# A two-layer encoder trunk: turning the output between the layers on VectorE and through device memory instead of on TensorE

## The chip, the cores and the metric

The kernel runs on one core of one Trainium2 chip. The metric is the device time of one launch in microseconds. One core has TensorE (matrix multiplications into PSUM; its weight loads are listed apart as PEld), VectorE (DVE), ScalarE (ACT), GpSimd (POOL), and SyncE (SP), which here issues most transfers between device memory and the on-chip memory SBUF. The engines run side by side, each through its own instructions in order, and wait for one another by semaphores.

## The reference

A trunk of two layers over one sequence of 256 rows and 2048 columns, in float32. Each layer is one mixer with three head groups fed by one input projection, then a residual and a LayerNorm:

```python
def hybrid_layer(x, mem, w_in, rel_table, gate_w, gate_b, gla_norm_g, w_mem_kv, w_out, ln_g, ln_b):
    h = x @ w_in
    a_q, a_k, a_v, a_z, b_q, b_k, b_v, b_z, b_lr, m_q, m_z = jnp.split(h, cuts, axis=-1)
    y_a = chunk_band_attention(a_q, a_k, a_v, rel_table)
    o_b = gla_chunk_recurrence(b_q, b_k, b_v, log_g)          # log_g from b_lr; then an RMS norm
    mk, mv = jnp.split(mem @ w_mem_kv, 2, axis=-1)
    y_m = memory_attention(m_q, mk, mv)
    y = concat([y_a * silu(a_z), y_b * silu(b_z), y_m * silu(m_z)])
    return layer_norm(DEEPNORM_ALPHA * x + y @ w_out, ln_g, ln_b)

def reference(x, mem, ...):
    h = x
    for l in range(2):
        h = hybrid_layer(h, mem, w_in[l], ...)
    return h
```

(Reshapes and some arguments are left out.) What matters here is the seam between the layers: the output of layer 0 is both the input of the big projection of layer 1 and its residual.

## The kernel before

**Products.** Every float32 operand is split into a high part (a cast to float32r) and a low part (the remainder), and a product is made of three matmuls: high by high, low by high, high by low. ScalarE makes the high part and VectorE the low part (`parts`, L114 to L117). All matmuls are recorded at L93.

**Weights.** The weights stream from device memory in pieces of 128 partitions x 1024 elements (512 KB), one per call of `piece` (L128 to L143): a load by SyncE into a `raw` buffer, then `wh` by ScalarE and `wl` by VectorE. There are four buffers each of `raw`, `wh` and `wl`. A piece is 16 or so matmuls. Groups of eight pieces follow each other; `as_group` puts the activations on the stationary side, `ws_group` the weights (two halves of four pieces).

**Order.** The orders of TensorE and SyncE are the order of the program text (L49); those of ScalarE and VectorE are planned when the kernel is built, where `piece` has a high priority (AHEAD, 4000) and `transposed` one of AHEAD // 4 for its scaling and splitting. Small jobs such as attention heads are generators: `tick` runs the next step of a waiting one after each weight piece, and the number that a step yields is how many pieces later the next one is due. At most two are active at once.

**The seam.** After the last output group of layer 0, `norm_between` (L627 to L642) normalises the sum in place in `res` (two tiles of 128 rows x 2048 columns) without the LayerNorm's gain and offset. Layer 1 then runs group MV of the memory projection (`as_group`, eight pieces), group MK (`ws_group`, eight pieces), and BQK, the first group that multiplies the layer's own input. For that input the columns have to lie on the partitions: 16 blocks of 128 columns, four to a quarter, each quarter an `operand` (`xq[q]`) of high and low parts. Five such operand buffers exist, and the four of the memory input `memq` are still read by MK.

`transposed` (L574 to L600) does the turning, started just ahead of MK and finished before BQK (L779, `finish(gens[:1])`). It first turns gain and offset into per-partition columns (`gT`, L578 and L579). Then in each of eight steps TensorE turns four blocks of 128x128 of `res` into a PSUM bank (L590), ScalarE and VectorE scale them with gain and offset into a scratch buffer (L596, L598), and `parts` writes the quarter's high and low halves. One step follows each MK piece. `restored` later applies gain and offset to `res` itself for the residual (L607, L608).

Of the kernel before, what the change touches and what calls it, by code (L numbers as in the profile page):

```python
# [8 lines left out]
F32 = mybir.dt.float32  # L9
# [3 lines left out]
AF = mybir.ActivationFunctionType  # L13
ALU = mybir.AluOpType
# [4 lines left out]
P = 128  # L19
D = 2048  # L20
T = 256
# [11 lines left out]
AHEAD = 4000  # L33
# [3 lines left out]
def hybrid_trunk_kernel(  # L37
# [7 lines left out]
    pe, dve, act, pool, sp = nc.tensor, nc.vector, nc.scalar, nc.gpsimd, nc.sync  # L45
# [27 lines left out]
    def enter(name, bufs=1, **kw):  # L73
        return ctx.enter_context(tc.tile_pool(name=name, bufs=bufs, **kw))
# [4 lines left out]
    wp = enter("wp", 4)  # L79
    hd = enter("hd", 1)  # L80
    sc = enter("sc", 8)
    sm = enter("sm", 1)
    psd = enter("psd", 2, space=bass.MemoryType.PSUM)
    psa = enter("psa", 4, space=bass.MemoryType.PSUM)

    uid = [0]

    def nm(s):
        uid[0] += 1
        return f"{s}_{uid[0]}"  # L90
# [4 lines left out]
    def bank():  # L95
        return psa.tile([P, 512], F32, name=nm("bk"), tag="bk")

    def scratch(shape, dtype=F32):
        return sc.tile(shape, dtype, name=nm("sc"), tag="sc")
# [4 lines left out]
    ident = cst.tile([P, P], F32, name="ident")  # L104
    lmask = cst.tile([P, 6, CH], U8, name="lmask")
    eye = cst.tile([P, CH], F32, name="eye")
    eps = cst.tile([P, 2], F32, name="eps")

    def operand():

        x = opp.tile([P, 4, 2, T], F32R, name=nm("x"), tag="x")
        return x[:, :, 0], x[:, :, 1], x.rearrange("p j h t -> p j (h t)")

    def parts(hi, lo, src):  # L114

        act.copy(hi, src)  # L116
        dve.tensor_tensor(lo, src, hi.bitcast(F32), op=ALU.subtract)  # L117
# [456 lines left out]
    def transposed(xq, gbT):  # L574

        raw, gT = gbT
        pt = bank()
        pe.transpose(pt[:, :P], raw, ident)  # L578
        dve.tensor_copy(gT, pt[:, :32])  # L579
        for q in range(4):  # L580
            x = operand()
            hi, lo, _ = x
            xq.append(x)
            for j in range(0, 4, 2):
                pt = bank()
                y = scratch([P, 2, T])
                for jj in range(2):
                    kt = q * 4 + j + jj
                    for t in range(2):
                        pe.transpose(pt[:, jj * T + t * P:jj * T + (t + 1) * P], res[:, t, kt * P:(kt + 1) * P], ident)  # L590
                with tc.high_priority(AHEAD // 4):
                    for jj in range(2):
                        kt = q * 4 + j + jj
                        src, g, b = pt[:, jj * T:(jj + 1) * T], gT[:, kt:kt + 1], gT[:, 16 + kt:17 + kt]
                        if jj == 0:
                            act.activation(y[:, jj], src, AF.Identity, bias=b, scale=g)  # L596
                        else:
                            dve.tensor_scalar(y[:, jj], src, g, b, op0=ALU.mult, op1=ALU.add)  # L598
                    parts(hi[:, j:j + 2], lo[:, j:j + 2], y)
                yield 1  # L600

    def restored(gb):

# [10 lines left out]
    def wo_pieces(l, n):  # L614

        if n < 3:
            return [w512[l, G_WO + n, pc] for pc in range(8)]
        return [[w256[l, i, pc // 2][:, pc % 2 * 512:pc % 2 * 512 + 512] for i in range(2)] for pc in range(8)]
# [137 lines left out]
    res = per.tile([P, 2, D], F32, name="res")  # L756
# [3 lines left out]
    for l in range(L):  # L760
        mk = [per.tile([P, 4, T], F32R, name=nm("mk"), tag=f"mk{i}") for i in range(2)]
        mv = [per.tile([P, 2, 512], F32R, name=nm("mv"), tag=f"mv{i}") for i in range(2)]
        xq = []
        if l == 0:
            def each(p):
                if p in (2, 4, 6, 7):
                    xq.append(resident_quarter(len(xq), xT[len(xq)]))

            first_memory(mk, mv, each)
        else:  # L770
            memq = []
            parts(*mv, as_group(w512[l, G_MV], memq, 512, 2, memT))
            gens = [transposed(xq, gbT), restored(gb)]
            waiting.append(gens[0])
            for i, a, b in ws_group(w512[l, G_MK], memq):
                tmp = scratch([P, 2, T])
                total(tmp, a, b)
                parts(mk[0][:, i:i + 2], mk[1][:, i:i + 2], tmp)
            finish(gens[:1])  # L779
# [21 lines left out]
        def heads(g):  # L801
            t = hd.tile([P, 4, T], F32, name=nm("qk"), tag="qk", bufs=4)
            for i, a, b in ws_group(w512[l, g], xq):
                total(t[:, i:i + 2], a, b)
            return t
# [12 lines left out]
        bias = {}  # L818
# [12 lines left out]
        for half in range(2):  # L831
            values(2 + half)
            q = heads(G_AQ0 if half == 0 else G_AQ1)
            k = heads(G_AK0 if half == 0 else G_AK1)
            gens.append([a_head(half * 4 + h, load_bias, bias, q[:, h], k[:, h], asv, yraw[1 + half][:, h]) for h in range(4)])
            waiting.extend(gens[-1])
        q = [hd.tile([P, 4, T], F32R, name=nm("mq"), tag="qk", bufs=4) for _ in range(2)]
# [15 lines left out]
        for i, g in ((1, G_AZ0), (2, G_AZ1), (3, G_MZ)):  # L853
            y = operand()
# [18 lines left out]
        for n in range(WO_N):  # L873
            if last:
                g, b = scratch([P, 512]), scratch([P, 512])
            else:
                both = per.tile([P, 2, 512], F32, name=nm("gb"), tag=f"yr{n}")
                g, b = both[:, 0], both[:, 1]
# [3 lines left out]
            src = wo_pieces(l, n)  # L882
# [122 lines left out]
```

## Time and profile before

| | |
|---|---|
| time of three runs, median (lowest to highest) | 925.73 us (925.34 to 926.28) |
| the profiled execution's own time | 925.59 us |
| its span, from first to last instruction | 923.8 us |
| granted TensorE clock, mean | 0.998 |
| bytes read and written in device memory | 175.77 MB and 2.10 MB |
| the eight steps of turning on TensorE (L590) | 482.3 to 505.6 us |

The time of an execution is 1.8 us more than its span. The profile lists for each engine how long it was busy, and a chain of work followed back from the last instruction: at each step to what released it, or to the instruction before it on its engine. Rows of a group give `out<-in`, partitions x elements, a count, busy time, the mean time of one in ns, and the idle time before them with what ended it. In a timeline the first number is the start in us from the span's start and the second the duration. "SPq" is the queue of instructions of SyncE. DMA rows give the size and the median time from issue to landing.

### The profile page before, as it was taken

How to read it: one execution, taken by the hardware profiler on the slowest of the kernel's cores; microseconds unless marked ns; L12 is line 12 of the kernel's file. 1: busy time of each engine (PE TensorE's matmuls, PEld its weight loads, DVE VectorE, ACT ScalarE, POOL GpSimd, SP SyncE). 2: the span in 40 equal slices, each digit the busy share in tenths (PEclk: the TensorE clock that was granted, in tenths of full speed). 3: DMA queues.
4: the chain of work that ended last, by engine and by line, in shares of the span. 5: the costliest groups of instructions: out<-in, count | busy, mean ns of one | idle time of the engine just before them, and what ended most of it. 6: DMA issues, size and time to landing. Idle time of an engine off the chain costs nothing.

```text
span 923.8 us, 14249 instructions
## 1 busy us (share of the span) xinstructions
PE 916.7 (99%) x5500; PEld 806.5 (87%) x5500; DVE 587.9 (64%) x812; ACT 498.2 (54%) x714; POOL 21.8 (2%) x49
## 2 busy tenths in 40 slices
PE   9999999999999999999999999999999999999997
PEld 7889998998888888888888899889888888888885
DVE  6764478665564666555587666975655555766566
ACT  6644485484454675433566445754744555754350
POOL 1000000000000000000000000000000000110000
PEclk9999999999999999999999999999999999999999
DMA  9955865546554566756675466546555544667652
GB/s 306 334 189 174 306 207 173 161 165 194 183 162 160 171 206 200 219 193 196 227 249 164 150 205 204 193 154 196 170 193 166 164 152 160 199 222 223 198 163 92
DMA packets 71253, 178.85 MB, mean 194 GB/s; under 512 B 7304, under 2 KB 31240, under 8 KB 70928
## 3 DMA queue, kind: packets, MB, share of 16 engines
q1 hardware_dynamic: 69120, 173.30, 57.1%
q0 software_dynamic: 1920, 4.36, 1.8%
q8 instruction: 43, 0.70, 0.3%
q10 hardware_dynamic: 144, 0.26, 0.1%
q14 instruction: 26, 0.21, 0.1%
HBM read 175.77 MB, written 2.10 MB: 193 GB/s over the span
## 4 chain that ended last, share of the span: by engine, by line
PE 98%; DMA 0%; DVE 0%; ACT 0%; SPq 0%; issue 0%
PE acc L93 89%; PE bk L93 8%; PE bk L526 1%; DMA raw<-w 0%; PE bk L561 0%; PE bk L590 0%; PE bk L494 0%; PE bk L393 0%; SPq L177 0%; ACT res L746 0%; ACT wh L116 0%; DVE stats L731 0%; PE bk L340 0%; DVE res L730 0%; DVE res L682 0%
## 5 line engine op out<-in xcount | busy, mean ns | idle before, releaser
L117 DVE TENSOR_TENSOR wl<-raw,wh 128x1024 fp32r<-128x1024 f32 (+3 forms) x321 | 370.0, 1154 | 255.9 <-ACT wh L116 254.9
L116 ACT CAST wh<-raw 128x1024 fp32r<-128x1024 f32 (+3 forms) x321 | 318.7, 994 | 329.9 <-PE acc L93 236.5
L93 PE MATMUL acc<-x,wh 128*128 128x512 f32 x1248 | 398.0, 400 | 0.1
L93 PE MATMUL acc<-wh,x 128*128 128x512 f32 (+2 forms) x1236 | 357.3, 370 | 0.1
L93 PEld LDWEIGHTS acc<-x,wl 128*128 128x128 f32 x1248 | 234.4, 188 | 55.3
L93 PEld LDWEIGHTS acc<-wh,x 128*128 128x128 f32 x1236 | 227.0, 188 | 27.9 <-ACT wh L116 0.6
L93 PE MATMUL acc<-x,wl 128*128 128x256 f32 x1248 | 246.0, 278 | 0.0
L93 PE MATMUL acc<-wl,x 128*128 128x512 f32 (+2 forms) x618 | 228.0, 369 | 0.0
L93 PEld LDWEIGHTS acc<-x,wh 128*128 128x128 f32 x1248 | 192.0, 189 | 1.9 <-ACT wh L116 0.4
L93 PEld LDWEIGHTS acc<-wl,x 128*128 128x128 f32 x618 | 116.0, 188 | 15.0 <-DVE wl L117 0.9
L518 ACT ACTIVATE sc<-sc,mx 128x128 f32<-128x128 f32 (+1 forms) x32 | 14.4, 450 | 20.3 <-DVE mx L516 20.3
L511 DVE SCALAR_TENSOR_TENSOR sc<-bk,bias 128x384 f32<-128x384 f32 x16 | 8.9, 554 | 12.7 <-PE bk L93 12.7
L382 ACT ACTIVATE sc<-sc 128x512 f32<-128x512 f32 x12 | 7.6, 633 | 12.5 <-DVE sc L380 12.5
L117 DVE TENSOR_TENSOR x<-sc,x 128x512 fp32r<-128x512 f32 x20 | 13.3, 684 | 0.7 <-ACT x L116 0.7
L116 ACT CAST x<-raw 128x1024 fp32r<-128x1024 f32 x5 | 5.3, 1053 | 15.3 <-DMA raw<-memT 12.7
L117 DVE TENSOR_TENSOR x<-res,x 128x512 fp32r<-128x512 f32 (+2 forms) x14 | 10.5, 765 | 4.2 <-ACT x L116 4.1
L93 PE MATMUL bk<-qk,qk 128*128 128x128 f32 (+1 forms) x64 | 13.1, 326 | 0.0
L117 DVE TENSOR_TENSOR x<-raw,x 128x1024 fp32r<-128x1024 f32 x5 | 6.1, 1225 | 10.9 <-ACT x L116 10.9
L93 PE MATMUL bk<-sc,asv 128*128 128x256 f32 (+1 forms) x64 | 13.0, 326 | 0.0
L262 DVE SCALAR_TENSOR_TENSOR sc<-acc,sc 128x512 f32<-128x512 f32 x19 | 12.9, 681 | 0.0
L116 ACT CAST x<-sc 128x512 fp32r<-128x512 f32 x20 | 11.8, 615 | 1.3 <-DVE sc L598 1.3
L623 DVE SCALAR_TENSOR_TENSOR res<-res,acc 128x512 f32<-128x512 f32 x15 | 9.7, 684 | 4.2 <-PE acc L93 4.2
(209 smaller groups left out, 567.8 us busy)
## 6 DMA issues: line engine op xcount, KB each, us to landing
raw<-w SPq DMA_DIRECT2D x214, 512.0 KB, 3.9
raw<-w SPq DMA_DIRECT2D x64, 388.0 KB, 3.3
raw<-w SPq DMA_DIRECT2D x83, 256.0 KB, 3.2
bias<-relw SPq DMA_DIRECT2D x16, 192.0 KB, 4.1
res<-xT SPq DMA_DIRECT2D x4, 512.0 KB, 5.0
res<-xn SPq DMA_DIRECT2D x1, 2048.0 KB, 8.2
raw<-memT SPq DMA_DIRECT2D x4, 512.0 KB, 4.3
res<-memT SPq DMA_DIRECT2D x6, 256.0 KB, 6.1
```

The lines of the kernel that those rows point to most:

```text
L93: pe.matmul(o, l, r, start=start, stop=stop, skip_group_check=True)
L116: act.copy(hi, src)
L117: dve.tensor_tensor(lo, src, hi.bitcast(F32), op=ALU.subtract)
L262: dve.scalar_tensor_tensor(dst, a, scale, dst, op0=ALU.mult, op1=ALU.add)
L382: act.activation(dd, dd, AF.Abs)
L511: dve.scalar_tensor_tensor(s, pb[:, :384], SCALE, bias[h], op0=ALU.mult, op1=ALU.add)
L518: act.activation(s[:, own[t]], s[:, own[t]], AF.Exp, bias=mx[:, t:t + 1], accum_out=zs[:, t:t + 1])
L526: pe.transpose(pt[:, i * P:(i + 1) * P], s[:, i * P:(i + 1) * P], ident)
L623: dve.scalar_tensor_tensor(r, r, ALPHA, acc, op0=ALU.mult, op1=ALU.add)
```

## The change

In `transposed` the 32 turns of 128x128 on TensorE go. In their place:

- In its first step VectorE turns `res` in blocks of 32x32 within each group of 32 partitions: four instructions, each 128 partitions x 1024 elements, into four tiles `turned` (which share the four buffers of tag `qk`).
- Two and three pieces later SyncE writes these tiles to a scratch tensor `blocks` in device memory, in sixteen transfers of 32 partitions x 1024 elements (128 KB, rows of 2 KB), eight for each half of the rows of `res`. The addresses put each 32x32 block where it belongs in the full turn.
- In each of the four steps after that SyncE reads one quarter back, 128 partitions x 8 x 128 elements (512 KB, rows of 512 B), into a `raw` buffer, one of the four that the weight pieces use. ScalarE and VectorE scale it in place with gain and offset, and `parts` writes the operand as before.

```diff
@@ -82,6 +82,7 @@
     psa = enter("psa", 4, space=bass.MemoryType.PSUM)
+    drm = enter("drm", 1, space=bass.MemoryType.DRAM)
@@ -105,6 +106,7 @@
     eps = cst.tile([P, 2], F32, name="eps")
+    blocks = drm.tile([P, 8, 512], F32, name="blocks")
@@ -577,27 +579,37 @@
         pt = bank()
         pe.transpose(pt[:, :P], raw, ident)
         dve.tensor_copy(gT, pt[:, :32])
+        turned = {}
+        for t in range(2):
+            for c in range(2):
+                turned[t, c] = hd.tile([P, 2, 16, 32], F32, name=nm("turn"), tag="qk", bufs=4)
+                dve.transpose(turned[t, c].rearrange("p b k j -> p k b j"),
+                              res[:, t].rearrange("p (k b j) -> p k b j", b=4, j=32)[:, :, 2 * c:2 * c + 2])
+        yield 2
+        for t in range(2):
+            for c in range(2):
+                for a in range(4):
+                    sp.dma_start(blocks[c * 64:c * 64 + 64, t * 4 + a].rearrange("(b i) n -> i b n", b=2),
+                                 turned[t, c][a * 32:a * 32 + 32].rearrange("p b k j -> p b (k j)"))
+            yield 1
         for q in range(4):
-            x = operand()
-            hi, lo, _ = x
-            xq.append(x)
-            for j in range(0, 4, 2):
-                pt = bank()
-                y = scratch([P, 2, T])
-                for jj in range(2):
-                    kt = q * 4 + j + jj
-                    for t in range(2):
-                        pe.transpose(pt[:, jj * T + t * P:jj * T + (t + 1) * P], res[:, t, kt * P:(kt + 1) * P], ident)
-                with tc.high_priority(AHEAD // 4):
-                    for jj in range(2):
-                        kt = q * 4 + j + jj
-                        src, g, b = pt[:, jj * T:(jj + 1) * T], gT[:, kt:kt + 1], gT[:, 16 + kt:17 + kt]
-                        if jj == 0:
-                            act.activation(y[:, jj], src, AF.Identity, bias=b, scale=g)
-                        else:
-                            dve.tensor_scalar(y[:, jj], src, g, b, op0=ALU.mult, op1=ALU.add)
-                    parts(hi[:, j:j + 2], lo[:, j:j + 2], y)
-                yield 1
+            with tc.high_priority(AHEAD // 4):
+                raws = wp.tile([P, 8, 128], F32, name=nm("raw"), tag="raw")
+                sp.dma_start(raws, blocks[:, :, q * 128:(q + 1) * 128])
+                x = operand()
+                hi, lo, _ = x
+                xq.append(x)
+                y = raws.rearrange("p g (k j) -> p k g j", j=32)
+                for j in range(4):
+                    kt = q * 4 + j
+                    g, b = gT[:, kt:kt + 1], gT[:, 16 + kt:17 + kt]
+                    if j % 2 == 0:
+                        act.activation(y[:, j], y[:, j], AF.Identity, bias=b, scale=g)
+                    else:
+                        dve.tensor_scalar(y[:, j], y[:, j], g, b, op0=ALU.mult, op1=ALU.add)
+                for j in range(0, 4, 2):
+                    parts(*(z[:, j:j + 2].rearrange("p k (g j) -> p k g j", j=32) for z in (hi, lo)), y[:, j:j + 2])
+            yield 1
```

On SyncE, in the order of the built kernel, the first eight writes stand between the loads of the third and fourth piece of MK, the other eight between those of the fourth and fifth, and the four reads behind the loads of the fifth to eighth piece.

## The prediction

> **What bounds the kernel now.** I read the page's busy times and its chain of work first, then the chain, the timelines and the waits around the place of the change, then the DMA rows.
>
> ```profile
> span 923.8 us, 14249 instructions
> PE 916.7 (99%) x5500; PEld 806.5 (87%) x5500; DVE 587.9 (64%) x812; ACT 498.2 (54%) x714; POOL 21.8 (2%) x49
> PE 98%; DMA 0%; DVE 0%; ACT 0%; SPq 0%; issue 0%
> ```
>
> TensorE is busy without a break and 98% of the chain that ended last is its own work. So a microsecond taken from TensorE is a microsecond gained, and a microsecond in which it waits for data is a microsecond lost. The chain around the change:
>
> ```profile
> by line: PE acc L93 93.3%; PE bk L590 7.0%; PE bk L578 0.2%
> 469.79 12.53 PE acc L93 x59
> 482.32 0.11 PE bk L578
> 482.43 0.44 PE bk L590 x4
> 482.87 2.79 PE acc L93 x16
> ...
> 502.30 2.80 PE acc L93 x16
> 505.11 0.44 PE bk L590 x4
> 505.54 14.53 PE acc L93 x83
> ```
>
> Each row of 16 is one weight piece of group MK; I call them MK0 to MK7, and Q0 to Q7 the pieces of the next group (BQK), which is the first to read the turned output. Behind each MK piece stand four turns (L590), eight times 0.44 us. What feeds TensorE there:
>
> ```profile
> 479.38 0.62 PE L93 MATMUL acc<-x,wh 128*128 128x512 f32 x2
> 479.83 0.40 PE L93 MATMUL acc<-x,wl 128*128 128x256 f32 x2
> 474.40 1.22 DVE L117 TENSOR_TENSOR wl<-raw,wh 128x1024 fp32r<-128x1024 f32 x1
> 476.48 3.50 DVE L117 TENSOR_TENSOR wl<-raw,wh 128x1024 fp32r<-128x1024 f32 x3 [0.85 <-ACT wh L116]
> SPq L141 <- DVE wl L117: 56.6, 27, 3.0
> ACT wh L116 <- PE acc L93: 21.1, 17, 1.9
> ```
>
> MK0 starts at 479.4 and wants its low part (wl) at 479.8; VectorE had made those of MK0, MK1 and MK2 from 476.5 to 480.0. The last two rows (waits, 430 to 530 for SyncE, 470 to 530 for the rest) say what paces the feeders: SyncE's loads wait for VectorE to give a raw buffer back, and ScalarE's high parts wait for TensorE to give a wh buffer back. There are four of each, so loads are in time by several pieces, but only while SyncE's queue moves.
>
> **The change part by part.**
>
> **Removed:** 32 turns on TensorE, 8 x 0.44 = 3.5 us off the path. L578 (0.11) stays.
>
> **Added on VectorE:** four block turns of 1024 elements per partition. In the order in which the changed kernel is built they stand right behind the low part of the last MV piece and ahead of those of MK0, MK1 and MK2.
>
> ```profile
> 472.57 1.92 DVE L642 TENSOR_SCALAR res<-res,rstd,nmr 128x512 f32<-128x512 f32 x4
> 472.57 2.94 ACT L640 ACTIVATE res<-res,nmr,rstd 128x512 f32<-128x512 f32 x4 [0.61 <-DVE nmr L635]
> 475.41 2.93 ACT L116 CAST wh<-raw 128x1024 fp32r<-128x1024 f32 x3
> ```
>
> Their input is ready at 475.5 (end of L640) and VectorE is free at 475.6. No row has a block turn. Below, L642 does 512 elements in 0.48, so 1024 in 0.96; above, twice the 1.17 of a 1024-element subtraction (3.50 / 3), 2.3. I take 1.15, the subtraction's, the nearest in shape. The four end at 480.2, MK0's low part at 481.4, wanted at 479.8: TensorE waits **1.5 us** (0.8 to 6.1; but at the upper end the later waits shrink, and the sum below grows by only 1.5).
>
> **Added on SyncE:** sixteen writes of 128 KB and four reads of 512 KB, placed between the loads of MK2 and Q0.
>
> ```profile
> L141 SPq DMA_DIRECT2D raw<-w x272: 327/328/423, 38.0 to 872.8; - x136
> raw<-w SPq DMA_DIRECT2D x214, 512.0 KB, 3.9
> out<-res SPq DMA_DIRECT2D x6, 256.0 KB, 2.4
> out<-res SPq DMA_DIRECT2D x2, 128.0 KB, 1.9
> DMA packets 4547, 4.90 MB, mean 196 GB/s; under 512 B 283, under 2 KB 4379, under 8 KB 4545
> q1 hardware_dynamic: 4545, 4.88, 61.5%
> DMA packets 1927, 6.78 MB, mean 226 GB/s; under 512 B 241, under 2 KB 289, under 8 KB 1925
> q1 hardware_dynamic: 1829, 6.70, 66.7%
> ```
>
> An issue costs SyncE 0.33. A store of 256 KB takes 0.5 more than one of 128 KB, so a write is 0.5 of transfer and 1.4 of latency. For the reads, the last two pairs are the DMA views of 420 to 445 (mostly 1 KB rows) and 470 to 500 (4 KB rows): 0.615 x 16 x 25 / 4545 = 54 ns for 1.07 KB and 0.667 x 16 x 30 / 1829 = 175 ns for 3.66 KB, that is 47 ns per KB and 4 ns per packet. A 512 KB load is then 1.57 of transfer, and 2.0 of its 3.9 is latency; a read in 1024 rows of 512 B is an estimated 1.82.
>
> Now the queue. The first turned tile is there at 476.7, so SyncE issues the first eight writes from 476.8 to 479.4, then MK3's load, which queues behind 4 us of writes and lands at 484.6. The last of the next eight writes shares a completion semaphore with MK3's load and waits for it: issued 484.6, landed 487.7. Behind it stands MK4's load, issued at 485.0 and landed at 490.1. MK4's two parts (1.05 and 1.17) are done at 492.4, and TensorE, 1.5 late, wants the low part at 492.6. Just covered.
>
> The first read waits for all sixteen writes: 487.7 + 0.33 + 2.0 + 1.82 lands it at 492.0; MK5's load behind it at 493.5, the second read at 495.3. MK5's low part is done at 495.8 and wanted at 495.4: **0.5**. MK6's load needs MK4's buffer, lands at 496.9, its cast on ScalarE stands behind the second quarter's two scalings and a PSUM eviction, and the low part is done at 499.2, wanted at 498.6: **0.6**.
>
> MK7 is where it gives. (Which buffer a load takes is read from the waits in the built order.) Its load takes the first read's buffer, which is free at 497.2, for the last subtraction of the first quarter stands behind the scaling of the second on VectorE. It lands at 501.5. And on VectorE the scaling of the fourth quarter stands ahead of MK7's low part. That quarter's read takes MK6's buffer (499.2), lands at 503.3, is scaled by 504.0, and MK7's low part is done at 505.2, while TensorE wants it at 502.0: **3.2**.
>
> ```profile
> 497.42 1.28 DVE L117 TENSOR_TENSOR x<-sc,x 128x512 fp32r<-128x512 f32 x2
> 496.14 1.14 ACT L116 CAST x<-sc 128x512 fp32r<-128x512 f32 x2
> ```
>
> Q0 follows at once: ScalarE has the third and fourth quarter's casts (2 x 1.14 with the wait between) ahead of Q0's, and Q0's parts are done at 508.0 and 509.2 where TensorE could have begun at 507.6: **1.2**. From there every load has its buffer early again (1.6 us of transfer per 2.8 us of matmuls).
>
> Sum of the waits: 1.5 + 0.5 + 0.6 + 3.2 + 1.2 = 7.0. Net 7.0 - 3.5 = +3.5: the span goes from 923.8 to 927.3, the profiled execution from 925.59 to 929.1, and the median from 925.73 to **929.2**. The scaling and splitting of the quarters replaces as much work of the same engines; reading SBUF instead of PSUM gains nothing on the path, because what ends the waits is a landing.
>
> Ends of the unknown prices, carried through the same steps: writes at the pace of the busy 1 KB reads (0.41) 5.6 us of waits, at twice 0.5, since each comes from 32 partitions and the stores from 128, 15.0; reads as fast as 4 KB rows 6.6, at twice their time 12.9; turns 6.8 and 8.5. All low, with latency 0.5 shorter, 3.8. I keep 0.5 for a write, the row nearest in kind.
>
> [...]
>
> **The rivals.**
>
> **The writes are the bound.** If a write takes 1.0, sixteen are 16 us of transfer in front of the first read, MK3 and MK4 come late by 1.1 and 6.8, waits are 15.0 and the time is 937.2. For it: all 16 stand in one queue with the weights, 32 partitions each. Against it: the DMA engines are busy 67% here, and the 128 KB store at the end took 1.9 in all.
>
> **Faster: the round trip is covered.** Place: SyncE's queue from MK2 to Q0. If every landing from the first write to the fourth read comes sooner, so that the fourth is in by 500.1 rather than 503.3, the waits at MK5, MK6, MK7 and Q0 go and only the turns' 1.5 stays: 925.73 - 3.5 + 1.5 = 923.7. It decides from 3.2 us less over three round trips in series, some 1.1 each. For it: buffers of four and loads well ahead. Against it: 1.9 was the least store, and the order on VectorE puts the scalings ahead of the weights.
>
> **The clock falls.** A wait of 3.2 us may cost more than itself.
>
> ```profile
> 918.00:921.00 3.00, 0.65 (x3) 0.73 0.70 251
> ```
>
> At the end of the kernel, with TensorE busy 0.65 of 3 us, the granted clock is 0.73. If it fell to half after MK7 for as long as that wait, 3.2 us, another 1.6 would go: 930.8. Against it: MK7's first matmuls cut the wait in two, so no gap exceeds 1.8. [...]
>
> **How the numbers follow.** Two runs of this kernel can be told apart from 0.2%, 1.9 us. The forecast's chain, 927.0 to 932.5, gets 0.57; slow writes or reads, 932.5 to 939, 0.2; the clock 0.07 (within the forecast's range); the covered round trip 0.16, of which 0.1 is below 923.9 and the rest within 0.2%. Of the forecast's share 0.09 lies below 927.6. So faster 0.1, same 0.15, slower 0.75. The range runs from 925.5 (all prices low and a little more) to 937 (one price doubled).
>
> **What would show it.** L590 gone and no 0.44 rows in the chain. Four block turns on VectorE at 475.6 and TensorE waiting for MK0's low part until about 481.4. The last write landing near 487.7 and the first read near 492. TensorE waiting on wl just ahead of the first Q piece, about 3 us, with the fourth read as what ended it. Wrong if TensorE shows no wait between 490 and 510, if a block turn is 2 us or more, if a write takes over 4 us to land with the queue free, or if time is lost after 530, where I place nothing.

## The result and the profile after

| | before | after |
|---|---|---|
| four runs each on one chip, median (lowest to highest) | 925.97 us (925.34 to 926.28) | 933.00 us (929.98 to 933.61) |
| ratio of the times, 95% interval | | 1.0070 (1.0048 to 1.0093) |
| profiled execution, its span | 925.59, 923.8 us | 933.61, 931.8 us |
| granted TensorE clock, mean | 0.998 | 0.994 |

The kernel is slower by 7.0 us, twice the +3.5 forecast, and inside the range. The page of the changed kernel, its totals and its chain by engine:

```profile
span 931.8 us, 14220 instructions
PE 918.1 (99%) x5468; PEld 805.7 (86%) x5468; DVE 591.0 (63%) x816; ACT 498.7 (54%) x714; POOL 21.9 (2%) x49
PE 91%; DMA 5%; DVE 2%; ACT 1%; issue 1%; SPq 1%; DVEq 0%
```

TensorE has 32 matmuls less and yet 1.4 us more busy time, and its share of the chain fell from 98% to 91%: waits have come in, and part of the busy time is matmuls that run longer (a pair of `wh` matmuls took 1.05 us from 509.07 and 0.63 from 515.13). SyncE's queue around the change (start, duration, count):

```profile
476.85 3.67 SPq L592 DMA_DIRECT2D blocks<-turn  x8
480.62 0.39 SPq L143 DMA_DIRECT2D raw<-w  x1
481.11 4.90 SPq L592 DMA_DIRECT2D blocks<-turn  x8
486.10 0.38 SPq L143 DMA_DIRECT2D raw<-w  x1
490.02 0.61 SPq L598 DMA_DIRECT2D raw<-blocks  x1
490.69 0.64 SPq L143 DMA_DIRECT2D raw<-w  x1
```

The sixteen writes occupy the queue until 486.0, then comes MK4's load; the next instruction is the first read, which waits for the last write's landing (at 489.75) and is issued at 490.02, and behind it stands MK5's load (490.69). The chain shows the same stretch with the landings as durations, and where it returns to TensorE:

```profile
480.62 5.07 DMA raw<-w
485.69 0.02 issue
485.70 4.05 DMA blocks<-turn
...
491.37 7.03 DMA raw<-blocks
498.42 1.09 ACT raw L607 x2
...
502.22 4.24 DMA raw<-blocks
...
508.48 11.58 PE acc L94 x49
```

The first row is MK3's load: the last write waits for its landing at 485.69 and leaves at 485.70. The last write lands at 489.75, the second read at 498.4, the fourth at 506.5. What TensorE makes of it is in its timeline; these are all its rows from 480 to 514 that have a wait in front (in brackets: its length and what ended it):

```profile
481.36 0.50 PE L94 MATMUL acc<-x,wl 128*128 128x256 f32 x2 [0.58 <-DVE wl L119]
493.42 0.50 PE L94 MATMUL acc<-x,wl 128*128 128x256 f32 x2 [0.51 <-DVE wl L119]
497.23 0.73 PE L94 MATMUL acc<-x,wh 128*128 128x512 f32 x2 [1.22 <-ACT wh L118]
498.49 0.50 PE L94 MATMUL acc<-x,wl 128*128 128x256 f32 x2 [0.53 <-DVE wl L119]
502.25 0.51 PE L94 MATMUL acc<-x,wl 128*128 128x256 f32 x2 [0.53 <-DVE wl L119]
506.00 0.73 PE L94 MATMUL acc<-x,wh 128*128 128x512 f32 x2 [1.14 <-ACT wh L118]
508.48 0.80 PE L94 MATMUL acc<-x,wl 128*128 128x256 f32 x2 [1.75 <-DVE wl L119]
```

They belong to MK0, MK4, MK5 (two), MK6 and MK7 (two). And windows of 1 or 2 us around the last pair (TensorE's busy time and count stand first, then the other engines'; behind the five engines stands the granted clock, then DMA share and GB/s):

```profile
504.00:506.00 2.00, 0.86 (x7) 0.56 (x5) 1.29 (x2) 2.00 (x4) 0.00 (x0) 1.00 0.76 222
507.00:508.00 1.00, 0.00 (x0) 0.00 (x0) 1.00 (x2) 1.00 (x3) 0.00 (x0) 0.93 0.69 274
508.00:509.00 1.00, 0.52 (x2) 0.52 (x3) 1.00 (x3) 1.00 (x2) 0.00 (x0) 0.50 0.50 201
514.00:515.00 1.00, 1.00 (x5) 0.86 (x5) 0.88 (x2) 0.84 (x1) 0.00 (x0) 0.66 1.00 324
515.00:516.00 1.00, 1.00 (x8) 0.91 (x7) 0.76 (x1) 0.49 (x2) 0.00 (x0) 1.00 0.95 389
```

TensorE's clock is at half from about 507.9 to 514.7, 6.8 us. A window of 1 us in which TensorE is busy throughout holds 4 or 5 matmul rows at 0.50 (the five from 509 to 514) and 8 at the full clock (515 to 516): half a clock looks like full work, which is why the page's busy share hides it.

### The profile page after: what moved, and what is told of

It is laid out like the page before. It is cut to its first block, busy times and chain, and to the rows that moved or that the text cites. A ratio compares the mean times of both kernels' runs of the same rounds, so it can differ in the third digit from the quotient of the medians.

```text
span 931.8 us, 14220 instructions
## 1 busy us (share of the span) xinstructions
PE 918.1 (99%) x5468; PEld 805.7 (86%) x5468; DVE 591.0 (63%) x816; ACT 498.7 (54%) x714; POOL 21.9 (2%) x49
## 4 chain that ended last, share of the span: by engine, by line
PE 91%; DMA 5%; DVE 2%; ACT 1%; issue 1%; SPq 1%; DVEq 0%
PE acc L94 82%; PE bk L94 7%; DMA raw<-memT 2%; DMA raw<-blocks 1%; DMA raw<-w 1%; DVE wl L119 1%; PE bk L528 1%; DMA blocks<-turn 0%; PE bk L563 0%; ACT wh L118 0%; ACT x L118 0%; ACT res L652 0%; DVE x L119 0%; DVE turn L586 0%; PE bk L496 0%
## 5 line engine op out<-in xcount | busy, mean ns | idle before, releaser
L119 DVE TENSOR_TENSOR x<-raw,x 128x512 fp32r<-128x512 f32 (+1 forms) x13 | 11.2, 888 | 13.2 <-ACT x L118 13.2
L118 ACT CAST x<-raw 128x512 fp32r<-128x512 f32 (+1 forms) x13 | 9.9, 779 | 15.3 <-DMA raw<-memT 12.1
L94 PEld LDWEIGHTS bk<-sc,asv 128*128 128x128 f32 x64 | 11.3, 189 | 1.2
L637 DVE BATCH_NORM_STATS2 stats<-res 128x6 f32<-128x256 f32 x31 | 11.4, 415 | 0.1
```

The source lines that it names most:

```text
L94: pe.matmul(o, l, r, start=start, stop=stop, skip_group_check=True)
L637: dve.bn_stats(stats[:, t, 2 * n + i], r[:, i * 256:(i + 1) * 256])
```

## The experiments

Each line is a median against the kernel before on the same chip (its medians were 925.9 to 926.1):

| run | what differs | us | ratio, 95% interval |
|---|---|---|---|
| x2_noturn | before, no turns on TensorE | 922.26 | 0.9964 (0.9951 to 0.9976) |
| x3_turns | before, block turns added | 926.99 | 1.0011 (1.0002 to 1.0020) |
| x10_wonly | x2, block turns and writes added | 925.50 | 0.9995 (0.9986 to 1.0004) |
| x1_fill | after, TensorE kept busy in its waits | 930.38 | 1.0048 (1.0035 to 1.0060) |
| x4_own | after, reads into other buffers | 929.81 | 1.0043 (1.0030 to 1.0056) |
| x11_late | x4, scaling queued later | 928.43 | 1.0027 (1.0018 to 1.0036) |
| x5_pool | x4, reads issued by GpSimd | 927.49 | 1.0019 (1.0010 to 1.0028) |
| x18_spread | x4, writes spread between the loads | 929.88 | 1.0042 (1.0028 to 1.0055) |
| x20_early | x18, two turns behind MK0's low part | 930.40 | 1.0045 (1.0033 to 1.0058) |
| x12_all | x5, scaling later, turns later | 934.53 | 1.0103 (1.0084 to 1.0122) |
| x13_eight | after, eight writes of 256 KB | 947.03 | 1.0218 (1.0204 to 1.0232) |
| x15_best | x13 with x4 and two moves | 942.22 | 1.0176 (1.0162 to 1.0190) |

### What TensorE gets back: x2_noturn

```diff
-                for jj in range(2):
-                    kt = q * 4 + j + jj
-                    for t in range(2):
-                        pe.transpose(pt[:, jj * T + t * P:jj * T + (t + 1) * P], res[:, t, kt * P:(kt + 1) * P], ident)
...
-                        src, g, b = pt[:, jj * T:(jj + 1) * T], gT[:, kt:kt + 1], gT[:, 16 + kt:17 + kt]
+                        src, g, b = res[:, :, kt * P:(kt + 1) * P], gT[:, kt:kt + 1], gT[:, 16 + kt:17 + kt]
```

> The kernel before without its turns between the layers: the quarters are scaled straight from the result in SBUF, unturned, so this leaves that turn out. It measures what TensorE gets back at most. Theory of the prediction: 32 transposes of 0.11 us leave TensorE, 3.5 us, and no wait comes: 925.9 - 3.5 = 922.4 (922.0 to 922.8). Rival: the transposes filled time in which TensorE would wait anyway (for the scaling's statistics or MK4's operands), and less than 2 us come back, 924 or more.

925.89 - 922.26 = 3.6 us: all of the turns' time comes back. 922.3 is the time from which the changed kernel's losses are counted: 933.0 - 922.3 = 10.7 us.

### The block turns alone: x3_turns

```diff
         dve.tensor_copy(gT, pt[:, :32])
+        turned = {}
+        for t in range(2):
+            for c in range(2):
+                turned[t, c] = hd.tile([P, 2, 16, 32], F32, name=nm("turn"), tag="qk", bufs=4)
+                dve.transpose(turned[t, c].rearrange("p b k j -> p k b j"),
+                              res[:, t].rearrange("p (k b j) -> p k b j", b=4, j=32)[:, :, 2 * c:2 * c + 2])
```

> The kernel before plus the four block turns on VectorE alone, their results read by nothing; the turns on TensorE stay. It measures the block turns' part. Theory of the prediction: the four turns (4.6 us together on VectorE) stand ahead of MK0's low part, MK0 waits some 0.6 to 1.5 us, nothing later: 925.9 + 1 = 927 (926.4 to 927.6). Rival: the turns' delay of VectorE passes on to the scaling of the quarters too, 928 or more. Other rival: they are hidden, 925.9.

1.1 us. TensorE's only new wait is 1.04 us, at MK0's low part; the scaling of the quarters on VectorE begins 2.5 us later (486.8 and not 484.3), but TensorE waits for none of it.

### Turns and writes, no reads: x10_wonly

```diff
+        yield 2
+        for t in range(2):
+            for c in range(2):
+                for a in range(4):
+                    sp.dma_start(blocks[c * 64:c * 64 + 64, t * 4 + a].rearrange("(b i) n -> i b n", b=2),
+                                 turned[t, c][a * 32:a * 32 + 32].rearrange("p b k j -> p b (k j)"))
+            yield 1
```

> The kernel of x2_noturn (no turns on TensorE, quarters scaled unturned from the result in SBUF; this leaves that turn out) plus the four block turns and the sixteen writes, which nothing reads back. It gives the price of turns and writes together without the reads; the turns alone cost 1.1 us in x3_turns, x2_noturn measured 922.26. Theory A, the writes cost what the changed kernel shows at MK4 (its load issued at 486.1 behind the writes, 0.5 to 0.7 us of wait) and the rest of the loss is the reads': 922.3 + 1.1 + 0.6 = 924.0 (923.3 to 924.8). Rival B, the writes' issue on SP and their traffic make MK5 and MK6 late too: 925.5 or more. Rival C, the writes cost nothing without the reads: 923.4.

925.50 - 922.26 - 1.10 = 2.1 us for the writes, more than expected, and, apart from the turns' wait at MK0, at a single place. TensorE's waits from 476 to 530 in this kernel:

```profile
481.89 0.50 PE L94 MATMUL acc<-x,wl 128*128 128x256 f32 x2 [1.50 <-DVE wl L119]
493.94 0.74 PE L94 MATMUL acc<-x,wh 128*128 128x512 f32 x2 [0.96 <-ACT wh L118]
495.20 0.50 PE L94 MATMUL acc<-x,wl 128*128 128x256 f32 x2 [0.52 <-DVE wl L119]
```

The second pair is MK4. Its load left SyncE at 486.67, as soon as the writes were issued, and took 6.1 us to land, with two more loads, held up by the same writes, issued within 0.9 us behind it; in x4_own, where the next transfer left 2.8 us behind it, it took 4.7. Rival B's late MK5 and MK6 did not show: from 495.2 TensorE runs without a wait.

### The clock: x1_fill

```diff
             xh, _, both = xq[pc]
+            more = dict(fill).get(p0 + pc, (0, 0))
+            for _ in range(more[0]):
+                mm(spare, ident, res[:, 0, :512], True, True)
             for j in range(4):
...
+                for _ in range(more[1] if j == 0 else 0):
+                    mm(spare, ident, res[:, 0, :512], True, True)
...
-            for i, a, b in ws_group(w512[l, G_MK], memq):
+            spare = bank()
+            for i, a, b in ws_group(w512[l, G_MK], memq, {5: (1, 0), 7: (1, 2)}):
```

> The changed kernel with four spare matmuls of 128x128 by 128x512 (f32) on TensorE into a bank that nothing reads: one ahead of MK5, one ahead of MK7, two between MK7's first products. The changed kernel's trace shows the granted clock at 0.50 from 508 to 514 us, behind waits of TensorE between 504.7 and 508.4 us; the loss by that clock was 2.9 us and the loss by waits 8.0 us against 3.6 saved. Theory A, the idle time itself lowers the clock: with TensorE busy in the waits the windows from 508 to 515 show 1.00, the waits before the spare matmuls are filled but the pieces begin no earlier, and the time is about 933.0 - 2.9 = 930.1 (929 to 930.8). Rival B, the clock falls there for a reason that has nothing to do with the waits: still 0.50 for some 7 us, and 933 or, with the spare matmuls in the way, up to 935. Rival C, the waits are longer than what the spare matmuls fill and the clock falls all the same, somewhat later.

Adding four matmuls made the kernel faster, 930.38 against 933.00. The intervals of the two ratios overlap by 0.001, so the profile has to decide; the windows where the changed kernel was at half clock, here:

```profile
506.00:507.00 1.00, 0.99 (x5) 0.52 (x4) 1.00 (x3) 0.66 (x2) 0.00 (x0) 1.00 0.63 254
507.00:508.00 1.00, 1.00 (x7) 0.83 (x7) 0.63 (x2) 0.80 (x1) 0.00 (x0) 1.00 0.50 90
508.00:509.00 1.00, 1.00 (x8) 0.91 (x7) 0.72 (x1) 1.00 (x3) 0.00 (x0) 1.00 0.96 348
```

The clock stays at 1.00. The other executions agree: the mean clock was 0.998 or 0.999 in all five of this kernel and 0.994 or 0.996 in all four of the changed one. Theory A holds: the half clock is a consequence of TensorE's idle time. It costs about 2.6 us (933.0 - 930.4), a rough figure, since the four times of the changed kernel spread over 3.6 us.

### Three causes of the late pieces: x4_own, x11_late, x5_pool

x4_own takes the reads out of the ring of raw buffers:

```diff
-                raws = wp.tile([P, 8, 128], F32, name=nm("raw"), tag="raw")
+                raws = hd.tile([P, 8, 128], F32, name=nm("back"), tag="qk", bufs=4)
```

> The changed kernel with one edit: the four reads back land in buffers of the kind qk (those of the scaled and turned data) and not in the ring of raw buffers that the weight loads share. Theory of the prediction for MK7: its weight load waits for the first read's raw buffer; with that gone MK7's wait of 3.3 us falls below 1, the clock has no such gap to fall behind (2.9), while MK4's to MK6's waits (some 3.6) stay, since the writes and the wait for them on SP's queue stay: 933.0 - 2.3 - 2.9 = 927.8 (926.5 to 930). Rival, the writes and SP's queue set all of it: MK7's weight load is still issued behind the reads on SP's queue, its wait stays at 2 to 3.3 us and the time at 932 to 933.5.

MK7's wait went from 2.9 to 0.18 us, as the ring theory said, and the time fell by 3.2 us, less than forecast: MK5's wait grew, and now the clock fell behind that. TensorE's rows at MK5 and the windows behind them:

```profile
497.19 0.73 PE L94 MATMUL acc<-x,wh 128*128 128x512 f32 x2 [1.58 <-ACT wh L118]
498.45 0.50 PE L94 MATMUL acc<-x,wl 128*128 128x256 f32 x2 [0.53 <-DVE wl L119]
```

```profile
498.00:499.00 1.00, 0.55 (x3) 0.54 (x4) 1.00 (x4) 1.00 (x3) 0.00 (x0) 1.00 1.16 343
499.00:500.00 1.00, 1.00 (x5) 0.88 (x4) 1.00 (x3) 1.00 (x2) 0.00 (x0) 0.51 1.07 364
502.00:503.00 1.00, 1.00 (x6) 0.91 (x5) 1.00 (x4) 1.00 (x3) 0.00 (x0) 0.78 1.08 392
```

Two things stand ahead of MK5: its load waits on SyncE's queue behind the first read, which waits for the writes; and on ScalarE the first quarter's scaling stands ahead of its cast. x11_late moves the second alone:

```diff
+                q = step - 1
+                if q >= 0:
+                    with tc.issue_after(latest[0].ins), tc.issue_after(latest[1].ins):
+                        x = operand()
```

(`latest` holds the cast and the subtraction of the newest weight piece; a quarter is scaled one step after its read.)

> As x4_own, and each quarter's scaling and casts on ScalarE and VectorE are queued behind the cast and the subtraction of a later piece than before (the first quarter's behind MK5's, the second's behind MK6's, the others' behind MK7's); the reads stay on SyncE's queue and are issued as in x4_own. It tells the two causes of MK5's wait apart the other way round than x5_pool. Theory A (SP's wait for the writes makes MK5's load itself late): MK5's waits of 1.58 and 0.53 us stay within 0.5, the clock falls behind them as in x4_own, 928.5 to 930.5. Rival B (the scaling ahead of MK5's cast): MK5's wait falls below 0.6, no half clock, 924 to 926.

MK5's waits stayed at 1.56 and 0.53 and the clock fell behind them: theory A. That is the profiled execution (928.92). The ten executions part in two: five with a mean clock of 0.995 to 0.997 took 928.75 to 930.09, five with 0.998 or 0.999 took 927.03 to 928.11, so the clock seems to have fallen in only half of them. That may be part of the 1.4 us by which the median beats x4_own; no row tells the rest. x5_pool moves the first cause alone:

```diff
-                sp.dma_start(raws, blocks[:, :, q * 128:(q + 1) * 128])
+                pool.dma_start(raws, blocks[:, :, q * 128:(q + 1) * 128])
```

> As x4_own (reads into buffers of their own), and the four reads issued on GpSimd's queue, so that SyncE's queue holds only weight loads and the sixteen writes. In x4_own SP stood from 486.2 to 488.6 us in its wait for the writes' landing, MK5's load was issued at 489.3 behind the first read and landed at 495.8, when TensorE already wanted MK5. Theory A, the wait for the writes on SP's queue makes MK5 late: with it gone MK5's load is issued by 487, lands by 493, MK5's waits (1.58 and 0.53 us) and the half clock behind them (some 1.9) go, MK0's and MK4's (about 1.1 and 0.6) stay: 922.3 + 1.7 = 924 (923.3 to 925.5). Rival B, it is the scaling of the first quarter, which stands ahead of MK5's cast on ScalarE and waits for the read: the read lands no earlier, ScalarE still waits for it, MK5 stays 1.5 to 3 us late: 927 to 930.

MK5's wait is gone (with the wait for the writes the first read's bytes have gone from in front of MK5's load too, and no run parts these two), but 927.49 is 3.5 above theory A's 924. TensorE's waits in x5_pool:

```profile
481.12 0.50 PE L94 MATMUL acc<-x,wl 128*128 128x256 f32 x2 [0.99 <-DVE wl L119]
493.53 0.73 PE L94 MATMUL acc<-x,wh 128*128 128x512 f32 x2 [1.33 <-ACT wh L118]
494.79 0.51 PE L94 MATMUL acc<-x,wl 128*128 128x256 f32 x2 [0.53 <-DVE wl L119]
509.34 0.73 PE L94 MATMUL acc<-x,wh 128*128 128x512 f32 x2 [0.46 <-DVE x L119]
515.89 0.74 PE L94 MATMUL acc<-x,wh 128*128 128x512 f32 x2 [0.48 <-DVE x L119]
```

MK4 is late as in x10_wonly: its load (486.08) took 6.3 us, with the next loads issued 0.4 and 0.9 us behind it, against 4.7 in x4_own. And the reads from GpSimd's queue took 7.8 to 12.8 us to land, so that two quarters were late for their Q pieces. Two small new waits in place of one large one; the clock stayed at 1.00.

### The loads' places in the queue: x18_spread, x20_early

```diff
                     sp.dma_start(blocks[c * 64:c * 64 + 64, t * 4 + a].rearrange("(b i) n -> i b n", b=2),
                                  turned[t, c][a * 32:a * 32 + 32].rearrange("p b k j -> p b (k j)"))
-            yield 1
+                yield 1
```

> The reads in buffers of their own, as x4_own (929.81), and the sixteen writes given to SyncE's queue four at a time, one group for each weight load (MK3 to MK6), so that no load stands behind more than four issues (some 1.7 us) and MK5's and MK6's loads stand ahead of the first read and of its wait for the writes' landing. Theory A, the loads' places in SP's queue made MK4 to MK7 late: MK5's wait (2.1 us in x4_own) and the half clock behind it go, MK4's too; MK0's (1.1 us, the four block turns) stays: 922.3 + 1.1 + 0.3 = 923.7 (923.2 to 925). Rival B, the writes' bytes and their 2 KB runs slow the loads wherever they stand: waits of 1.5 us or more at MK4 to MK6, 925.5 to 928. Rival C, the reads, later by two pieces, bring the first quarters late for the next group's pieces, due at 508 us: a wait on the cast of x there, 925 or more.

All of TensorE's waits from 476 to 530:

```profile
481.55 0.50 PE L94 MATMUL acc<-x,wl 128*128 128x256 f32 x2 [1.71 <-DVE wl L119]
506.73 1.07 PE L94 MATMUL acc<-x,wh 128*128 128x512 f32 x2 [2.96 <-ACT wh L118]
507.99 0.80 PE L94 MATMUL acc<-x,wl 128*128 128x256 f32 x2 [0.19 <-DVE wl L119]
```

Rival B falls: with the same bytes in the same rows MK4 to MK7 have no wait at all, so it was the loads' places in the queue, behind the writes and the reads. But the time is 929.88, since the loss reappears at Q0 as one wait, with 3.4 us at half clock behind it. TensorE was through with MK7 at 503.77. Q0's load stands on SyncE's queue behind three reads, of which the last alone held the queue for 3.66 us:

```profile
492.97 5.01 SPq L598 DMA_DIRECT2D back<-blocks  x3
```

So Q0's load left at 498.02 and landed at 504.59, 0.8 us after TensorE had run dry. The rest is ScalarE's order:

```profile
501.59 1.09 ACT L607 ACTIVATE back<-back,gbT 128x256 f32<-128x256 f32 x2
502.58 0.61 ACT L118 CAST x<-back 128x512 fp32r<-128x512 f32 x1
503.09 0.62 ACT L118 CAST mk<-sc 128x512 fp32r<-128x512 f32 x1
503.62 1.09 ACT L607 ACTIVATE back<-back,gbT 128x256 f32<-128x256 f32 x2
504.61 1.12 ACT L118 CAST x<-back 128x512 fp32r<-128x512 f32 x2
505.64 1.99 ACT L118 CAST wh<-raw 128x1024 fp32r<-128x1024 f32 x2
```

ScalarE works without a gap, but the built order puts the fourth quarter's scaling (503.62) and the third quarter's casts (504.61) ahead of Q0's cast (the first of the two `wh`), which begins 1.05 us after its load has landed. Begun at the landing, it would have left an estimated 1.9 of the 2.96 us of wait. Rival C had the place, and not the cause: the first quarter's parts, which Q0 needs, were done at 502.2; late were the load behind the reads and the cast behind the other quarters. x20_early changes the turns' place and starts the writes a piece earlier:

```diff
-                dve.transpose(turned[t, c].rearrange("p b k j -> p k b j"),
-                              res[:, t].rearrange("p (k b j) -> p k b j", b=4, j=32)[:, :, 2 * c:2 * c + 2])
-        yield 2
+                with tc.issue_after(latest[1].ins) if t else ExitStack():
+                    dve.transpose(turned[t, c].rearrange("p b k j -> p k b j"),
+                                  res[:, t].rearrange("p (k b j) -> p k b j", b=4, j=32)[:, :, 2 * c:2 * c + 2])
+        yield 1
```

> As x18_spread, with the groups of writes one piece earlier and the last two block turns queued on VectorE behind MK0's low part. If MK0's wait comes from two of the four turns standing ahead of its low part, it goes (below 0.3 us), and with the others gone TensorE has its 3.5 us back: 922.3 to 923.5, below the kernel before (925.9) and at least 0.8 below x18_spread. Rival: MK1's or MK2's low part is late in MK0's place, or MK3's load, now behind four writes, makes MK3 wait: no better than x18_spread.

MK0's wait is gone, so it did come from the last two turns: its low part is done at 479.1, where TensorE wants it at 480.4; behind two more turns (2.4 us) it would have been late. But MK3 and MK4 wait 0.53 and 0.26, and MK6 2.21 and 1.25 us: in this order it is MK6's load that stands behind the first read, whose issue waited for the writes until 492.1. 930.40, no better.

### Misses: x12_all, x13_eight, x15_best

x12_all is x5_pool with the scaling one step later and this:

```diff
-                dve.transpose(turned[t, c].rearrange("p b k j -> p k b j"),
+                tc.keep_in_program_order(dve.transpose(turned[t, c].rearrange("p b k j -> p k b j"),
```

> Everything together: reads into buffers of their own and on GpSimd's queue, scaling queued behind a later piece, and the block turns kept in program order on VectorE, behind MK0's low part. If the theory holds, MK0's wait (1.1) goes, MK5's to MK7's too, and at most MK4's 0.6 is left: 922.3 + 0.6 = 922.9 (922.3 to 924), which is below the kernel before (925.9). Rival: the reads on GpSimd's queue land late, as the quarters are due at 508 us for the next pieces, and TensorE waits for the first quarter instead, 925 or more.

934.53. Program order put the turns not only behind MK0's low part but behind the copy of `gT`, which waits for TensorE: VectorE began them at 482.5 instead of 475.6, the writes went out from 483.7, MK3's load behind eight of them at 487.6, MK4's at 493.1, and TensorE waits 5.85 us at MK3 alone. (These figures are from the profiled execution, which took 939.53, 5.0 us above the median.)

x13_eight sends the same bytes as eight writes from 128 partitions each:

```diff
-                for a in range(4):
-                    sp.dma_start(blocks[c * 64:c * 64 + 64, t * 4 + a].rearrange("(b i) n -> i b n", b=2),
-                                 turned[t, c][a * 32:a * 32 + 32].rearrange("p b k j -> p b (k j)"))
+                for b in range(2):
+                    i0 = c * 64 + b * 32
+                    sp.dma_start(blocks[i0:i0 + 32, t * 4:t * 4 + 4].rearrange("i a n -> a i n"),
+                                 turned[t, c][:, b].rearrange("p k j -> p (k j)"))
```

> The changed kernel with the same 2 MB written by eight transfers of 256 KB from 128 partitions in place of sixteen of 128 KB from 32; nothing else is changed, the reads still land in the ring of raw buffers. x10_wonly showed turns and writes alone at 925.5, 2.1 us above the turns alone. Theory A, the writes hold SP's queue by their count (sixteen issues of 0.43 us) and land slowly from 32 partitions: eight issues take some 3.5 to 4 us, the last write lands near 486 instead of 489.8, MK4's load is issued by 483 and the first read and MK5's load by 487, MK4's and MK5's waits go and MK7's load, which follows the first read's buffer, comes 3 us earlier: only MK0's 1.1 us and some rest are left, 922.3 + 1.1 + 0.5 = 924 (923.3 to 925.5). Rival B, what counts is the bytes, which are the same: writes land as late as before, waits stay, 929 to 933.

947.03: both theories missed. Two windows while its writes are under way:

```profile
490.00:492.00 2.00, 0.39 (x3) 0.19 (x1) 0.00 (x0) 0.00 (x0) 0.00 (x0) 1.00 0.26 91
492.00:494.00 2.00, 0.00 (x0) 0.00 (x0) 0.00 (x0) 0.40 (x1) 0.00 (x0) 1.00 0.26 101
```

The DMA share stands at 0.26 and the rate near 100 GB/s, while the changed kernel reaches 199 to 273 GB/s, at a share of 0.93 or 0.94, from 478 to 481, when its first eight writes are under way. 0.26 of sixteen engines is the work of some four, and four is also the size of the write's outermost dimension in device memory (`a`), which is 32 (`i`) in the changed kernel's writes; that the one comes from the other is the author's estimate, for no run changes that dimension alone. So x13_eight measures a slow write and does not separate the number of writes from their bytes; the last one landed at 504.2. x15_best has the same writes, the reads in buffers of their own and one piece later, and the last two turns behind MK0's low part:

> Eight writes from 128 partitions, and three further edits: reads into buffers of their own (as x4_own), the last two block turns queued on VectorE behind MK0's low part, and the reads traced one piece later, so that MK5's load stands ahead of the first read and of its wait for the writes on SP's queue. If MK0's wait (1.1 us) comes from the four turns and MK5's from SP's wait for the writes, both go and no wait above 0.5 us is left: 922.3 + 0.5 = 922.8 (922.2 to 924), some 3 us below the kernel before. Rival: the reads, one piece later, bring the quarters late for the next group of pieces, or the scaling ahead of a later piece's cast holds that piece; then 924.5 to 928, no better than x13_eight.

942.22; its windows show the same share of 0.26 and 98 GB/s (490 to 494). No version measured here that turns the data fully beats the kernel before.

## Why the prediction came out as it did

**The saving** was right: 3.5 forecast, 3.6 measured (x2_noturn).

**The block turns** were right. Four took 4.61 us from 475.59 (4.6 from 475.6 forecast), and MK0's low part let TensorE go at 481.36 (481.4). The wait in that execution was 0.6 because TensorE reached MK0 0.8 later than in the execution before; alone the turns cost 1.1 (x3_turns). It is a wait that varies: in the profiled executions with all four turns ahead of MK0's low part it ran from none (x1_fill) to 1.71 us (x18_spread).

**The writes' issue** was mis-sized, and this is the first step that failed: "An issue costs SyncE 0.33". A write's issue took 0.42 (the median of sixteen), and the first eight held the queue for 3.67 us and not 2.6. So MK3's load went out 1.2 later and landed 1.1 later than forecast (485.69 and not 484.6), and the last write, which waits for that landing as forecast, left at 485.7. It then took 4.05 to land and not 3.1: 489.75 instead of 487.7. This second part belongs to the execution: in x1_fill, x4_own and x10_wonly the last write took 2.9 to 3.0. The other price, "a write is 0.5 of transfer and 1.4 of latency", held while the queue was free: the first write landed in 1.98 us, and the first eight landings came 0.55 apart on average (seven of the second eight came 0.33 apart). A read's issue took 0.53 to 0.61, again not 0.33. "MK4 ... Just covered" became 0.5 us, MK5's wait, forecast at 0.5, became 1.22 and 0.53, and the later landings keep the delay and add to it: the first read is late by 2.5 us, the second by 3.1, the fourth by 3.2. The read's own price held: 4.2 to 4.5 us for three of the four, 4.15 forecast (the second took 7.0).

**MK7** was right in kind and size: waits of 1.14 and 1.75, 2.9 us, against 3.2, ended by the fourth read and VectorE's order. x4_own confirmed that the ring of raw buffers causes it.

**The clock** is the second step that failed. The prediction had it as a rival at 0.07, with 1.6 us, and argued it away: "MK7's first matmuls cut the wait in two, so no gap exceeds 1.8". That the longest gap decides was an estimate; no gap exceeded 1.8 (the longest was 1.75), and the clock fell all the same, behind 3.4 us in which TensorE was busy for 1.1 (0.4 until 504.9 and the 0.73 from 506.0). The price was about 2.6 us, for the half clock lasted 6.8 us and not the 3.2 assumed. The clock is the larger part of the miss: the seven waits in TensorE's timeline add up to 6.3 us, against 7.0 forecast.

**Q0's 1.2** did not show: with MK7's rest at half clock (508.48 to 512.91, 4.4 us), Q0's parts were ready first. That the waits add up to nearly the forecast is in part luck: MK4 and MK5 took 1.8 us more than forecast, MK0 and Q0 2.1 less.

Together, from the medians: 1.1 for the turns, 2.1 for the writes, and 7.5 for reads and ring, of which the clock has some 2.6; 10.7 lost, 3.6 saved. That the parts add up so is an assumption: x4_own, x18_spread and x20_early show that a wait taken away at one piece comes back at another.

Of the other rivals, **the covered round trip** falls with the landings, which came later than forecast and not sooner, and **the writes are the bound** in its strong form (16 us of transfer) by x18_spread, where the same sixteen writes, spread over the queue, left MK4 to MK7 without a wait.

## What to carry to other kernels

A transfer that is free in bytes can be dear in place. Here what stood behind an issue, a landing or a buffer on SyncE's queue paid for it: in the changed kernel MK4's load left at 486.10 behind sixteen writes, and MK5's at 490.69 behind the last write's landing (489.75) and the first read. So list what stands behind a transfer before moving work to DMA. Where TensorE bounds the kernel, as here, look for a second price of a wait, the clock behind it (about 2.6 us here), and look for it in the busy share over a few microseconds, not in the longest gap: the clock held behind 1.71 us (x18_spread at MK0) and fell behind 1.58 and 0.53 (x4_own). And a repair is measured by the end of the kernel: x4_own, x5_pool, x18_spread and x20_early each removed the wait it aimed at, and none brought the time below the kernel before.

## What the runs showed of the hardware

In the profiled executions the clock went to half (0.50 in the windows) for about 3.4 us (x4_own, x11_late, x18_spread), for 6.8 (the changed kernel, x12_all, x13_eight, x20_early, and x15_best at 504.3), and once, in x15_best at 490.6, for 10.2. Where the windows of a trace show three changes or more near the seam, the times between them, worked out from the windows' mean clocks, are within 0.04 us of whole multiples of 3.41: 6.84 and 17.08 in x12_all, 6.84, 3.40 and 6.84 in x13_eight, 10.24, 3.44 and 6.80 in x15_best. In the changed kernel the clock fell at 507.85, rose at 514.68 (2 x 3.41 later) and fell again at the end of the kernel, at 927.69.

TensorE's busy time in the last 3.41 us before a fall, around the seam (475 to 530 us), was 1.14 us (the changed kernel), 1.31 (x4_own), 1.33 (x11_late) and at most 1.46 (x15_best). Counted in steps of 3.41 us from the falls, the clock held behind 1.71 (x18_spread at MK0) and 2.19 (the changed kernel at MK5). In x10_wonly it held where no 3.41 us had less than 1.9. It also held in x5_pool behind waits of 1.33 and 0.53 with 0.73 of matmuls between; how these lie to steps of 3.41 us no row shows, for that trace has no fall near the seam. So the longest gap does not decide alone: x4_own fell behind 1.58 and 0.53, x18_spread held behind 1.71. Nor does the busy time: at the end of the kernel before, the clock fell at 919.40 behind 2.04 us.
